# Reordering the mixer of a two-layer decoder step: conv half of the out product first, the S5 half last

## The chip, the cores and the metric

The kernel runs on one core of a Trainium2 chip. The metric is the device time of one execution in microseconds (us), the median of several runs. TensorE (PE in the profile) does the matrix products, VectorE (DVE) and ScalarE (ACT) the elementwise work, GpSimd (POOL) some copies and tables; SyncE (SP) and POOL issue the transfers.

## The reference, cut to what matters

Two layers over 288 token columns (a prompt of 256 and 8 samples of 4 tokens), model width 2048. The part of a layer that the change touches is the mixer:

```python
z = x @ w_in
u = z[..., :S5_WIDTH]
cv = z[..., S5_WIDTH:S5_WIDTH + CONV_WIDTH]
cg = z[..., S5_WIDTH + CONV_WIDTH:]
y5, h_re, h_im = _s5(u, h0_re, h0_im, ...)
g5 = jax.nn.gelu(y5.astype(x.dtype))
s5_out = g5 * jax.nn.sigmoid(g5 @ s5_w_glu)
c = cv * jax.nn.sigmoid(cg)
c, new_conv = _causal_dwconv(c, conv_buf, conv_w, conv_b)
c = jax.nn.silu(_ln(c, conv_ln_g, conv_ln_b))
mix = jnp.concatenate([s5_out, c], axis=-1) @ w_out
x = _ln(ALPHA * x + mix, ln1_g, ln1_b)
```

`_s5` is a scan over a diagonal complex state (64 groups); the convolution is 31 taps deep, its LayerNorm runs over all 1024 conv channels. A ConvFFN and an embedding stage follow, which the change leaves alone. All data are float32.

## The kernel before, in words

Tokens lie along the free dimension, features along the 128 partitions: `x32`, `xh` and `xl` are 16 tiles of 128 x 288 each. Every product is made of **blocks**: one 128 x 128 piece of a weight matrix times one such tile. Weights stream from memory in units of eight blocks (`wraw`, 512 KB); ACT and DVE split each unit into a high and a low part (`whi`, `wlo`), the activations are split the same way (`xh`, `xl`), and a block is three matmuls: whi·xh, whi·xl, wlo·xh (L369, L374, L375). A layer has 3104 blocks in the order of the table that `layer_phases` writes; the host packs the weights in that order, so PE, the splits and the weight transfers all follow it.

In the mixer the table runs: `u0` (64 blocks, the first four of eight chunks of `u`), then for each conv chunk j the pair `p{j}` (32 blocks: values and gates), with `v{j}` (16 blocks, one more chunk of `u`) behind p1 to p4, then `g` (64 blocks, the GLU product) and `o` (256 blocks, the whole out product, 16 columns over all 16 input tiles). I number the blocks of a layer from its start: u0 0 to 64, p0 64 to 96, p1 96 to 128, and so on.

Around them `mixer` writes out by hand:

* **The convolution of chunk j.** When p{j} is done, DVE makes the gated rows in `cbuf`; POOL writes them to memory (`cb_d`), loads the taps (`cw`) and reads the rows back in 32-row windows (`stack`, four transfers), writes them to the output (`out_dram<-cbuf`), and loads the next chunk's `cbuf`. There is one `cbuf`, one `cw` and one `stack`, so each waits for the last reader of the one before; the last chunk's `stack` is read by SP instead. `conv(j)` (64 small matmuls, L1105 and L1108) runs one chunk later, after p{j+1}; conv(7) after the first 32 blocks of `g`.
* **The S5 scan**, a background generator in steps: per chunk an injection (`bu`), a kernel product (`kps`), the scan on DVE, a projection (`y`), then GELU, a round through memory (`y_d`, back to `u32`) and a split. Its transfers (`ust`, `sqb`, `tm`, `k_d`, `y_d`) are issued by SP and POOL in program order between weight loads. Where its steps stand is decided while the program is written, by a clock `pe_t` that counts an assumed time for each block and each step of a convolution; `wait` and `at` put a step some thousand of these nanoseconds later.
* **The LayerNorm over the conv chunks** (`ln_finish`, then a pipeline of `ln_sub`, `c_norm`, `c_silu` and split per chunk): before, its small DVE chain has 24 blocks of `g` beside it, and the eight chunks' work the last of `g` and the first 40 blocks of `o`, which read the GLU's outputs.

`G_CUT = (32, 40, 64, 64)` says how `g` is cut around conv(7) and the LayerNorm. The GELU'd chunks lie in `xh[8..15]` before, the GLU's outputs in `xh[0..7]`; the conv half takes `xh[8..15]` after `g` has read them.

Of the kernel before, what the change touches and what calls it, by code (L numbers as in the profile page):

```python
# [7 lines left out]
F32 = mybir.dt.float32  # L8
F32R = mybir.dt.float32r
I32 = mybir.dt.int32  # L10
AF = mybir.ActivationFunctionType
OP = mybir.AluOpType

P = 128
DM = 2048
KD = DM // P
# [3 lines left out]
TOK = SEQ + NB * NT  # L20
# [6 lines left out]
CVC = 8  # L27
# [5 lines left out]
ALPHA = (2.0 * DEPTH) ** 0.25  # L33
# [8 lines left out]
STEP = 4  # L42
# [23 lines left out]
LOOK = 1  # L66
EV_GAP = 10
NATIVE = 10
G_CUT = (32, 40, 64, 64)
U_AT = {1: [4], 2: [5], 3: [6], 4: [7]}  # L70

PRM = {}
_o = 0
# [12 lines left out]
def _order(mat, ms, ks, g):  # L86
    ms, ks = list(ms), list(ks)
    out = [(mat, k, m) for k in ks for m in ms[:g]]
    for m in ms[g:]:
        out += [(mat, k, m) for k in ks]  # L90
    return out


def layer_phases():
    ph = [("u0", _order("w_in", range(4), range(KD), 4))]
    for j in range(CVC):
        ph.append((f"p{j}", _order("w_in", [8 + j, 16 + j], range(KD), 0)))
        if j in U_AT:
            ph.append((f"v{j}", _order("w_in", U_AT[j], range(KD), 0)))
    ph.append(("g", _order("s5_w_glu", range(8), range(8), 4)))  # L100
    ph.append(("o", _order("w_out", range(KD), range(KD), 5)))
    for z, ms in enumerate(EPARTS[:3]):
        ph.append((f"e{z}", _order("pe_w", ms, range(PEK), 0)))
    j0 = 0
    for h, n in enumerate(FH):
        ms = [m for j in range(j0, j0 + n) for m in (j, FF + j)]
        ph.append((f"up{h}", _order("ffn_w_up", ms, range(KD), 5 if h == 0 else 0)))
        ks = list(range(j0, j0 + n))
        dn = [("ffn_w_down", k, m) for m in (0, 1) for k in ks[:-2]]
        dn += [("ffn_w_down", k, m) for m in (0, 1) for k in ks[-2:]]  # L110
        dn += _order("ffn_w_down", range(2, KD), ks, 0)
        ph.append((f"dn{h}", dn))
        j0 += n
    for z, ms in enumerate(EPARTS[3:]):
        ph.append((f"e{3 + z}", _order("pe_w", ms, range(PEK), 0)))
    ph.append(("pg", _order("pe_w_gate", range(KD), range(KD), 5)))
    return ph
# [36 lines left out]
class Core:  # L154
# [188 lines left out]
    def run(self, blocks, xs, evac, sums=None, wide=False):  # L343

        nc = self.nc
        tot, seen, accs = sums or self.sums(blocks)
        k0, pend = blocks[0][1], []
        for _, k, m in blocks:
            if pend and k != k0:
                for out, w, xl in pend:  # L350
                    nc.tensor.matmul(out, w, xl, start=False, stop=False)  # L351
                pend = []
            w = self.next_block()
            if m not in accs:
                if wide and len(accs) == 4:
                    accs[m] = (1 << 30, self.ps.tile([P, 512], F32, tag="one", name="acc5", bufs=1))
                else:
                    t = self.acc_tile()
                    accs[m] = (self.acc_n, t)
            out = accs[m][1][:, :TOK]  # L360
            n = seen[m]
            first, last = n == 0, n == tot[m] - 1
            if len(w) == 1:
                self.pe_t += 485.0
                nc.tensor.matmul(out, w[0], self.x32[k], start=first, stop=last)
            else:
                xh, xl = xs(k)
                self.pe_t += 369.0
                nc.tensor.matmul(out, w[0], xh, start=first, stop=False)  # L369
                if k == k0 and not last and (pend or not seen[m]):  # L370
                    nc.tensor.matmul(out, w[1], xh, start=False, stop=False)  # L371
                    pend.append((out, w[0], xl))
                else:
                    nc.tensor.matmul(out, w[0], xl, start=False, stop=False)  # L374
                    nc.tensor.matmul(out, w[1], xh, start=False, stop=last)  # L375
            seen[m] += 1
            if last:
                a, t = accs.pop(m)
                self.evq.append((a, lambda m=m, t=t: evac(m, t[:, :TOK])))
            if self.evq and self.pos - self.ev_pos >= EV_GAP:  # L380
                self.evict()
        while self.evq:
            self.evict()
# [157 lines left out]
    def xs(self, k):  # L541
        self.need(k)
        return self.xh[k], self.xl[k]
# [507 lines left out]
    def mixer(self, l, ph):  # L1051
        nc, a = self.nc, self.a
        V = self.V
        with self.tc.tile_pool(name="mx", bufs=1) as mp:
# [3 lines left out]
            scan = self.scan = self.start(self.s5(l, mp), 0.0)  # L1058
# [8 lines left out]
            cst = self.ln_begin(CVC * P)  # L1067
# [19 lines left out]
            gsplit = set()  # L1087

            def split_g(force=False, n=S5C):
                while n and self.gdone and (force or self.gdone[0][1] <= self.pe_t):  # L1090
                    c = self.gdone.pop(0)[0]
                    self.split_x(8 + c, self.u32[c])
                    gsplit.add(c)
                    n -= 1

            def conv(j):
                st, cw = stacks.pop(j)
                o = self.acc_tile()
                for k in range(8):
                    self.tick()  # L1100
                    self.pe_t += 640.0
                    if j == CVC - 2 and k >= 4:
                        split_g(n=1)
                    for b in range(4):
                        nc.tensor.matmul(o[32 * b:32 * b + 32, :SEQ], cw[:, b, k], st[:, b, 4 * k:4 * k + SEQ],  # L1105
                                         start=(k == 0), stop=False, tile_position=(0, 32 * b))
                    for b in range(4):
                        nc.tensor.matmul(o[32 * b:32 * b + 32, SEQ:TOK], cw[:, b, k], window(st, b, CW + 4 * k),  # L1108
                                         start=False, stop=(k == 7), tile_position=(0, 32 * b))
                nc.scalar.activation(cvo[j], o[:, :TOK], AF.Identity, bias=self.prm("conv_b", j))  # L1110
                self.ln_acc(cst, cvo[j], j == CVC - 1)

            for j in range(CVC):
# [26 lines left out]
                if j:  # L1140
                    conv(j - 1)
                while "done" not in part:
                    self.late.pop(0)[1]()
                stack(j)
                if j in U_AT:
                    self.run(ph[f"v{j}"], self.xs, ev_u)

            def xs_g(k):
                split_g()
                while k not in gsplit:  # L1150
                    self.step(scan)
                    self.run_timed(True)
                    split_g(True)
                return self.xh[8 + k], self.xl[8 + k]
            def ev_g(m, acc):
                t = mp.tile([P, TOK], F32, tag="cvt", name="gt", bufs=3)
                nc.scalar.activation(t, acc, AF.Tanh, scale=0.25)
                w = mp.tile([P, TOK], F32, tag="cvt", name="gt", bufs=3)
                V.scalar_tensor_tensor(w.rearrange("p (n s) -> p s n", s=STEP),
                                       t.rearrange("p (s n) -> p s n", s=STEP), 1.0,  # L1160
                                       self.u32[m].rearrange("p (s n) -> p s n", s=STEP), op0=OP.add, op1=OP.mult)
                self.split_x(m, w, 0.25)
            sums = self.sums(ph["g"])
            self.run(ph["g"][:G_CUT[0]], xs_g, ev_g, sums)
            self.finish(scan)
            conv(CVC - 1)

            def fill(z):
                self.run(ph["g"][G_CUT[z]:G_CUT[z + 1]], xs_g, ev_g, sums)
            fill(0)  # L1170
            self.flush()
            self.ln_finish(cst, lambda z: z and fill(z), keep=True)
            th = {}

            def c_norm(j):
# [6 lines left out]
            def c_silu(j):  # L1182
# [2 lines left out]

            self.lazy(self.pipeline(CVC, ((0, lambda j: self.ln_sub(cst, cvo[j])), (1, c_norm), (2, c_silu),
                                          (3, lambda j: self.split_lo(8 + j, cvo[j], 0.5)))))
            if G_CUT[2] < G_CUT[3]:
                fill(2)
            self.load_p(l, mp)  # L1190
            st = self.ln_begin(DM)

            def xs_o(k):
                self.need(min(k - 3, 7) - LOOK)
                return self.xh[k], self.xl[k]

            def ev_o(m, acc):
                V.scalar_tensor_tensor(self.x32[m], self.x32[m], 1.0 if m == KD - 1 else ALPHA, acc,
                                       op0=OP.mult, op1=OP.add)
                self.ln_acc(st, self.x32[m], m == KD - 1)  # L1200
                if m == 6:
                    self.ln_pre(st, self.x32[KD - 1], ALPHA)
            self.run(ph["o"], xs_o, ev_o, wide=True)
        return st

    def load_p(self, l, mp):
# [307 lines left out]
```

## Time and profile before

| | |
|---|---|
| median of 3 runs | 2792.56 us (2791.43 to 2795.7) |
| the profiled execution's own time | 2793.7 us |
| its span, first to last instruction | 2791.9 us |
| PE busy in the span | 2684.0 us (96%) |
| DVE, ACT, POOL busy | 65%, 48%, 11% |
| mean granted TensorE clock | 0.984 of full speed |
| memory traffic | 463.27 MB read, 20.68 MB written |

A row of the "windows" view gives for a stretch of time how long each engine was busy in it and with how many instructions, the granted clock (1.00 is 2.4 GHz, 0.50 is 1.2 GHz), the busy share of the sixteen DMA engines and GB/s. In a row of the timeline the square bracket is the idle time of the engine just before, and what ended it. Layer one of the profile runs from 0 to about 1388 us, layer two from there; the first mixer ends near 415, the second near 1806.

### The profile page before, as it was taken

What the parts mean: (1) busy time and instruction counts of PE and PEld (TensorE: products, weight loads), DVE (VectorE), ACT (ScalarE), POOL (GpSimd) and SP (SyncE); (2) the same over time, 40 slices, a digit from 0 to 9 for tenths busy, and PEclk for the clock granted to TensorE, in tenths of its full rate; (3) what the DMA queues carried; (4) which work ended last, traced back from release to release, by engine and by line L of the source; (5) the groups of instructions that cost most, each with busy time, mean ns of one, the idle gap of its engine ahead of it and who ended that gap; (6) DMA issues with size and microseconds to landing.
All of it is one profiled execution on the core that took longest, in us unless ns stands there. A gap on an engine that the chain in (4) does not pass through costs nothing. (4 is left out here: it accounts for less than half of the span.)

```text
span 2791.9 us, 57891 instructions
## 1 busy us (share of the span) xinstructions
PE 2684.0 (96%) x23696; PEld 2623.0 (94%) x23696; DVE 1815.6 (65%) x3017; ACT 1353.2 (48%) x2224; POOL 304.3 (11%) x923
## 2 busy tenths in 40 slices
PE   8889999999999999999889879999999999999997
PEld 7778999999999999999888769999999999999997
DVE  6875768664566456667778747676645664566686
ACT  3444547553455345536454435475534553455363
POOL 3442001000000000000115410010000000000000
PEclk9999999999999999999999999999999999999998
DMA  7887544554455544544468874445555455455543
GB/s 238 240 237 224 171 152 164 162 181 163 158 168 164 180 159 157 181 162 151 145 197 242 225 206 156 150 161 165 180 166 162 159 179 171 150 173 171 166 152 102
DMA packets 175609, 487.72 MB, mean 175 GB/s; under 512 B 37616, under 2 KB 61696, under 8 KB 175344
## 3 DMA queue, kind: packets, MB, share of 16 engines
q1 hardware_dynamic: 160832, 434.56, 48.6%
q0 software_dynamic: 14512, 49.47, 6.4%
q8 instruction: 186, 3.05, 0.4%
q14 instruction: 79, 0.65, 0.1%
HBM read 463.27 MB, written 20.68 MB: 173 GB/s over the span
## 5 line engine op out<-in xcount | busy, mean ns | idle before, releaser
L369 PE MATMUL acc<-xh,whi 128*128 128x288 f32 x4656 | 1389.3, 299 | 13.0 <-ACT xh L528 5.1
L374 PE MATMUL acc<-xl,whi 128*128 128x288 f32 x4357 | 1289.7, 296 | 0.6 <-DVE xl L140 0.2
L375 PE MATMUL acc<-xh,wlo 128*128 128x288 f32 x4357 | 1284.3, 295 | 0.5 <-issue 0.5
L195 ACT ACTIVATE whi<-wraw 128x1024 fp32r<-128x1024 f32 x766 | 791.4, 1050 | 350.5 <-PE acc L374 220.4
L140 DVE TENSOR_TENSOR wlo<-wraw,whi 128x1024 fp32r<-128x1024 f32 x766 | 918.6, 1223 | 28.6 <-issue 12.5
L369 PEld LDWEIGHTS acc<-xh,whi 128*128 128x128 f32 x4656 | 876.5, 188 | 20.5 <-ACT xh L528 5.4
L374 PEld LDWEIGHTS acc<-xl,whi 128*128 128x128 f32 x4357 | 821.4, 189 | 3.7 <-DVE xl L140 2.1
L375 PEld LDWEIGHTS acc<-xh,wlo 128*128 128x128 f32 x4357 | 823.8, 189 | 0.7 <-issue 0.7
L140 DVE SCALAR_TENSOR_TENSOR fo<-fe,parf,fo 128x304 f32<-128x304 f32 x352 | 188.2, 535 | 354.2 <-ACT fo L1250 347.9
L369 PE MATMUL acc<-hh,whi 128*128 128x288 f32 x1408 | 416.4, 296 | 0.0
L374 PE MATMUL acc<-hl,whi 128*128 128x288 f32 x1312 | 387.7, 296 | 0.0
L375 PE MATMUL acc<-hh,wlo 128*128 128x288 f32 x1312 | 387.4, 295 | 0.0
L369 PEld LDWEIGHTS acc<-hh,whi 128*128 128x128 f32 x1408 | 264.9, 188 | 0.1
L375 PEld LDWEIGHTS acc<-hh,wlo 128*128 128x128 f32 x1312 | 247.2, 188 | 0.0
L374 PEld LDWEIGHTS acc<-hl,whi 128*128 128x128 f32 x1312 | 247.0, 188 | 0.0
L1246 ACT ACTIVATE fe<-acc 128x256 f32<-128x256 f32 x176 | 67.6, 384 | 301.1 <-PE acc L375 301.1
L1256 POOL COPY fstage<-fe 128x9 f32<-128x9 f32 x176 | 42.2, 240 | 1035.3 <-ACT fe L1247 1024.5
L428 ACT ACTIVATE ln_q<-x 128x288 f32<-128x288 f32 x90 | 40.2, 446 | 221.0 <-DVE x L140 221.0
L140 DVE TENSOR_TENSOR x<-x,acc 128x288 f32<-128x288 f32 x64 | 29.1, 454 | 144.7 <-PE acc L375 144.7
L1250 ACT ACTIVATE fo<-fe,parf 128x304 f32<-128x304 f32 x176 | 113.0, 642 | 16.5
L1270 ACT ACTIVATE hh<-fth 128x288 fp32r<-128x288 f32 x88 | 39.2, 445 | 162.9 <-DVE fth L140 162.9
L140 DVE SCALAR_TENSOR_TENSOR x<-x,acc 128x288 f32<-128x288 f32 x64 | 29.0, 453 | 132.9 <-PE acc L375 132.9
(237 smaller groups left out, 2366.9 us busy)
## 6 DMA issues: line engine op xcount, KB each, us to landing
wraw<-in_wts_dram SPq DMA_DIRECT2D x776, 512.0 KB
stack<-cb_d POOLq DMA_DIRECT2D x56, 282.0 KB, 8.8
cw<-in_convw_dram POOLq DMA_DIRECT2D x16, 512.0 KB, 5.7
cbuf<-in_convi_dram POOLq DMA_DIRECT2D x16, 283.5 KB, 4.5
cb_d<-cbuf POOLq DMA_DIRECT2D x16, 283.5 KB, 4.0
out_dram<-cbuf POOLq DMA_DIRECT2D x16, 283.5 KB, 10.4
tm<-k_d SPq DMA_DIRECT2D x64, 64.0 KB
sbt<-in_s5b_dram SPq DMA_DIRECT2D x14, 256.0 KB
```

The source lines that it names most:

```text
L140: return f(out, *args, **kw)
L195: self.nc.scalar.activation(hi, self.raw[s], AF.Copy)
L369: nc.tensor.matmul(out, w[0], xh, start=first, stop=False)
L374: nc.tensor.matmul(out, w[0], xl, start=False, stop=False)
L375: nc.tensor.matmul(out, w[1], xh, start=False, stop=last)
L428: nc.scalar.activation(st["q"], v, AF.Square)
L1246: nc.scalar.activation(e[:, 2:2 + SEQ], acc[:, :SEQ], AF.Copy)
L1250: nc.scalar.activation(o[:, :w], e[:, 2:EW], AF.Identity, bias=self.prm("ffn_conv_b", m), scale=self.prm("ffn_conv_w2", m))
L1256: nc.gpsimd.tensor_copy(stage[:, z, :, 0], e[:, SEQ:EW:6])
L1270: nc.scalar.activation(hh[i], h, AF.Copy, scale=0.5)
```

## The change

* `u` chunks 4, 5 and 6 follow p1, p2 and p5; chunk 7 (`vz`, 16 blocks) follows p7 and conv(6). conv(7) stands inside `vz`, after its sixth block, the LayerNorm's sums after its ninth.
* The out product is in two: `oc` (128 blocks, input tiles 8 to 15, the conv half) right after `vz`, then `g`, then `os` (128 blocks, the S5 half). `oc` adds into `alpha * x` (`ev_c`), `os` adds its result (`ev_s`): 16 more 128 x 288 additions per layer.
* The S5 chunk that takes its input from `vz` runs beside `oc`. The GELU'd chunks go to `xh[0..7]` and all eight are split where `g` begins, the GLU's outputs to `xh[8..15]`.
* `pe_t` counts 400 for a block (was 369) and 500 for a step of a convolution (was 640).

```diff
-G_CUT = (32, 40, 64, 64)
-U_AT = {1: [4], 2: [5], 3: [6], 4: [7]}
+U_AT = {1: [4], 2: [5], 5: [6]}
+U_END = 7
+V_CUT = (6, 9)
...
+    ph.append(("vz", _order("w_in", [U_END], range(KD), 0)))
+    ph.append(("oc", _order("w_out", range(KD), range(8, KD), 5)))
     ph.append(("g", _order("s5_w_glu", range(8), range(8), 4)))
-    ph.append(("o", _order("w_out", range(KD), range(KD), 5)))
+    ph.append(("os", _order("w_out", range(KD), range(8), 5)))
...
-                self.pe_t += 369.0
+                self.pe_t += 400.0
...
-                    self.split_x(8 + c, self.u32[c])
+                    self.split_x(c, self.u32[c])
...
-                    self.pe_t += 640.0
-                    if j == CVC - 2 and k >= 4:
-                        split_g(n=1)
+                    self.pe_t += 500.0
...
+            vz = ph["vz"]
+            vsum = self.sums(vz)
+            self.run(vz[:V_CUT[0]], self.xs, ev_u, vsum)
+            conv(CVC - 1)
+            self.run(vz[V_CUT[0]:V_CUT[1]], self.xs, ev_u, vsum)
+            self.flush()
+            self.ln_finish(cst, lambda z: z and self.run(vz[V_CUT[1]:], self.xs, ev_u, vsum), keep=True)
...
+            def ev_c(m, acc):
+                V.scalar_tensor_tensor(self.x32[m], self.x32[m], ALPHA, acc, op0=OP.mult, op1=OP.add)
+            self.run(ph["oc"], xs_c, ev_c, wide=True)
...
-                self.split_x(m, w, 0.25)
-            sums = self.sums(ph["g"])
-            self.run(ph["g"][:G_CUT[0]], xs_g, ev_g, sums)
+                self.split_x(8 + m, w, 0.25)
+            self.run(ph["g"], xs_g, ev_g)
             self.finish(scan)
-            conv(CVC - 1)
-
-            def fill(z):
-                self.run(ph["g"][G_CUT[z]:G_CUT[z + 1]], xs_g, ev_g, sums)
-            fill(0)
-            self.flush()
-            self.ln_finish(cst, lambda z: z and fill(z), keep=True)
...
-            def ev_o(m, acc):
-                V.scalar_tensor_tensor(self.x32[m], self.x32[m], 1.0 if m == KD - 1 else ALPHA, acc,
-                                       op0=OP.mult, op1=OP.add)
+            def ev_s(m, acc):
+                V.tensor_tensor(self.x32[m], self.x32[m], acc, OP.add)
                 self.ln_acc(st, self.x32[m], m == KD - 1)
...
-            self.run(ph["o"], xs_o, ev_o, wide=True)
+            self.run(ph["os"], lambda k: (self.xh[8 + k], self.xl[8 + k]), ev_s, wide=True)
```

What the table does to the engines' order is seen at three places of the second layer. The first is PE where the LayerNorm's last product (L510, L513 after the change) stands; `xh_102` is input tile 15, `xh_87` tile 0, `xh_95` tile 8. Before:

```order
L369 MATMUL acc<-xh_102,whi 128x288
L374 MATMUL acc<-xl_118,whi 128x288
L375 MATMUL acc<-xh_102,wlo 128x288
L510 MATMUL acc<-ln_dg,ones_120 128x288
L369 MATMUL acc<-xh_87,whi 128x288
L371 MATMUL acc<-xh_87,wlo 128x288
```

After:

```order
L378 MATMUL acc<-xh_101,wlo 128x288
L372 MATMUL acc<-xh_102,whi 128x288
L377 MATMUL acc<-xl_118,whi 128x288
L378 MATMUL acc<-xh_102,wlo 128x288
L513 MATMUL acc<-ln_dg,ones_120 128x288
L372 MATMUL acc<-xh_95,whi 128x288
L374 MATMUL acc<-xh_95,wlo 128x288
```

Before, the block behind that product reads a GLU output; now it reads conv chunk 0 after its normalisation.

The second is ACT around the LayerNorm's two copies (`ln_s<-acc`, L515 and L518); `gt` is the GLU's gate, `cvo` a conv chunk, `u_7` the last chunk of u. Before:

```order
L1157 ACTIVATE gt<-acc 128x288
L528 ACTIVATE xh_94<-gt 128x288
L515 ACTIVATE ln_s_20348<-acc 128x288
L515 ACTIVATE ln_s_20350<-acc 128x288
L1212 ACTIVATE phi<-p_20354 128x576
L195 ACTIVATE whi<-wraw 128x1024 x2
L1177 ACTIVATE cvo_16260<-ln_d,par 128x288
```

After:

```order
L1111 ACTIVATE cvo_16299<-acc,par 128x288
L431 ACTIVATE ln_q<-cvo_16299 128x288
L198 ACTIVATE whi<-wraw 128x1024
L1065 ACTIVATE u_7_16291<-acc 128x288
L518 ACTIVATE ln_s_19945<-acc 128x288
L518 ACTIVATE ln_s_19947<-acc 128x288
L198 ACTIVATE whi<-wraw 128x1024
L1160 ACTIVATE cvo_16292<-ln_d,par 128x288
L1162 ACTIVATE ln_d<-cvo_16292 128x288
L1160 ACTIVATE cvo_16293<-ln_d,par 128x288
L1162 ACTIVATE ln_d<-cvo_16293 128x288
L531 ACTIVATE xh_95<-cvo_16292 128x288
```

The copy of conv(7)'s result (`cvo_16299`), the LayerNorm and the first high part of the conv half (`xh_95`) now follow each other with two weight splits between them and no GLU work.

The third is POOL's queue behind conv(2), where `stack` of chunk 3 is read. Before:

```order
L1078 DMA stack<-cb_d 32x4x564 x4
L1080 DMA out_dram<-cbuf 128x567
L1064 DMA u_d_18349<-u_6_16258 128x288
L1115 DMA cbuf<-in_convi_dram 128x567
L864 DMA k_d<-kp 128x224
L926 COPY hin<-h_16275 128x4x8 x2
```

After:

```order
L1081 DMA stack<-cb_d 32x4x564 x4
L1083 DMA out_dram<-cbuf 128x567
L1116 DMA cbuf<-in_convi_dram 128x567
L867 DMA k_d<-kp 128x224
L929 COPY hin<-h_16307 128x4x8 x2
L889 TENSOR_TENSOR stb<-tix,fint 128x288
```

Chunk 6 of u has left this place with its 16 blocks; the load of the next `cbuf` now stands right behind the write that it has to wait for, and the S5 pieces behind it.

## Rows read from the trace of the kernel before

**Rows 1.** Windows: layer one from conv(0) to conv(7), and layer two's ConvFFN.

```profile
45.00:281.26 236.26, 208.50 (x3342) 188.61 (x3340) 167.57 (x291) 102.15 (x192) 98.12 (x172) 0.96 0.83 239
1810.00:2662.00 852.00, 852.00 (x6396) 851.51 (x6396) 514.47 (x766) 420.65 (x669) 48.38 (x267) 1.00 0.51 166
```

**Rows 2.** Windows, layer one: from conv(2) to conv(7), one row a chunk.

```profile
150.37:184.43 34.06, 30.66 (x562) 27.90 (x561) 26.46 (x45) 14.99 (x28) 12.59 (x25) 0.95 0.85 231
184.43:220.07 35.64, 29.64 (x449) 26.97 (x448) 28.00 (x49) 16.65 (x33) 19.60 (x30) 0.90 0.75 220
220.07:242.03 21.96, 20.63 (x402) 18.52 (x401) 13.72 (x26) 8.83 (x16) 6.16 (x15) 1.00 0.87 241
242.03:262.04 20.01, 18.95 (x321) 17.31 (x321) 7.37 (x11) 7.59 (x15) 4.26 (x9) 1.00 0.82 247
262.04:281.26 19.22, 17.33 (x225) 15.48 (x225) 9.30 (x17) 6.21 (x12) 3.24 (x6) 1.00 0.83 218
```

**Rows 3.** Windows, layer two: from conv(2) to conv(7), one row a chunk.

```profile
1525.47:1558.27 32.80, 30.03 (x514) 27.25 (x513) 26.91 (x51) 15.17 (x30) 15.89 (x28) 0.95 0.86 243
1558.27:1595.36 37.09, 31.92 (x561) 28.88 (x560) 28.18 (x47) 14.59 (x28) 12.42 (x25) 0.90 0.84 229
1595.36:1619.47 24.11, 21.00 (x401) 18.56 (x400) 19.17 (x35) 11.24 (x22) 10.81 (x20) 1.00 0.77 217
1619.47:1647.78 28.31, 20.69 (x322) 18.72 (x321) 7.55 (x11) 8.10 (x15) 5.84 (x13) 0.88 0.76 209
1647.78:1671.84 24.06, 18.93 (x225) 16.81 (x225) 11.33 (x22) 9.52 (x19) 2.70 (x5) 0.92 0.73 207
```

**Rows 4.** Waits of PE, 1560 to 1700 us: total us, times, longest.

```profile
PE y L389 <- DMA wraw<-in_wts_dram: 7.6, 1, 7.6
...
PE acc L369 <- ACT xh L528: 5.1, 1, 5.1
...
PE acc L369 <- ACT ln_s L515: 0.8, 1, 0.8
```

**Rows 5.** Chain that ended last, around conv(7) of layer two: start, us, what.

```profile
1652.91 7.66 DMA stack<-cb_d
1660.59 7.21 DMA u<-y_d
```

**Rows 6.** Timeline of PE: the first matmuls of conv(7) in layer one.

```profile
281.26 0.64 PE L1105 MATMUL acc<-stack,cw 128*32 128x256 f32 x8 [1.29 <-DMA stack<-cb_d]
```

**Rows 7.** Windows with L1105's matmuls alone: conv(6) of layer one.

```profile
262.04:266.30 4.26, 4.10 (x64) 1.30 (x64) 1.00 0.59 185
```

**Rows 8.** Timeline of POOL: loads of cbuf behind a write of it.

```profile
240.24 0.56 POOL L1115 DMA_DIRECT2D cbuf<-in_convi_dram  x1 [10.06 <-DMA out_dram<-cbuf]
1640.20 0.56 POOL L1115 DMA_DIRECT2D cbuf<-in_convi_dram  x1 [12.34 <-DMA out_dram<-cbuf]
```

**Rows 9.** Windows: two stretches at the lower clock, each behind a long wait.

```profile
1637.20:1643.90 6.70, 3.65 (x98) 3.49 (x99) 0.00 (x0) 0.49 (x2) 0.56 (x1) 0.50 0.79 223
1667.90:1674.60 6.70, 6.19 (x52) 4.36 (x56) 3.30 (x7) 2.85 (x8) 0.00 (x0) 0.50 0.10 42
```

**Rows 10.** Timeline of DVE and ACT: the conv LayerNorm of layer two.

```profile
1683.77 0.16 DVE L140 TENSOR_SCALAR ln_ne<-acc 96x6 f32<-96x6 f32 x1 [0.83 <-PE acc L459]
...
1686.30 0.45 DVE L140 SCALAR_TENSOR_TENSOR ln_dg<-ident,ln_n 96x288 f32<-96x288 f32 x1
1686.67 1.22 DVE L140 TENSOR_TENSOR wlo<-wraw,whi 128x1024 fp32r<-128x1024 f32 x1
...
1701.89 0.45 DVE L140 TENSOR_TENSOR ln_d<-cvo,ln_s 128x288 f32<-128x288 f32 x1
...
1704.39 0.43 ACT L528 ACTIVATE xh<-cvo 128x288 fp32r<-128x288 f32 x1
```

**Rows 11.** Lines of PE, 1440 to 1806 us: injections and the projections' second half.

```profile
L389 PE MATMUL y<-hin,om 128*32 128x72 f32 x512 | 15.6, 256 | 0.0
...
L389 PE MATMUL bu<-ust,em 128*32 128x72 f32 x448 | 10.6, 242 | 8.2 <-DMA ust<-u_d 5.2 <-ACT em L815 3.0
```

More of the change, by code (lines that the diff above doesn't have):

```diff
@@ L1146, in mixer @@
                     self.run(ph[f"v{j}"], self.xs, ev_u)
[L1148 to L1161, printed above, removed]
-                self.split_x(m, w, 0.25)
-            sums = self.sums(ph["g"])
-            self.run(ph["g"][:G_CUT[0]], xs_g, ev_g, sums)
-            self.finish(scan)
+            vz = ph["vz"]
+            vsum = self.sums(vz)
+            self.run(vz[:V_CUT[0]], self.xs, ev_u, vsum)
             conv(CVC - 1)
-            def fill(z):
-                self.run(ph["g"][G_CUT[z]:G_CUT[z + 1]], xs_g, ev_g, sums)
-            fill(0)
+            self.run(vz[V_CUT[0]:V_CUT[1]], self.xs, ev_u, vsum)
             self.flush()
-            self.ln_finish(cst, lambda z: z and fill(z), keep=True)
+            self.ln_finish(cst, lambda z: z and self.run(vz[V_CUT[1]:], self.xs, ev_u, vsum), keep=True)
             th = {}
@@ L1187, in mixer, with xs_c, xs_g, ev_g @@
                                           (3, lambda j: self.split_lo(8 + j, cvo[j], 0.5)))))
-            if G_CUT[2] < G_CUT[3]:
-                fill(2)
+            def xs_c(k):
+                self.need(k - 8)
+                return self.xh[k], self.xl[k]
+            def ev_c(m, acc):
+                V.scalar_tensor_tensor(self.x32[m], self.x32[m], ALPHA, acc, op0=OP.mult, op1=OP.add)
+            self.run(ph["oc"], xs_c, ev_c, wide=True)
+            def xs_g(k):
+                split_g()
+                while k not in gsplit:
+                    self.step(scan)
+                    self.run_timed(True)
+                    split_g(True)
+                return self.xh[k], self.xl[k]
+            def ev_g(m, acc):
+                t = mp.tile([P, TOK], F32, tag="cvt", name="gt", bufs=3)
+                nc.scalar.activation(t, acc, AF.Tanh, scale=0.25)
+                w = mp.tile([P, TOK], F32, tag="cvt", name="gt", bufs=3)
+                V.scalar_tensor_tensor(w.rearrange("p (n s) -> p s n", s=STEP),
+                                       t.rearrange("p (s n) -> p s n", s=STEP), 1.0,
+                                       self.u32[m].rearrange("p (s n) -> p s n", s=STEP), op0=OP.add, op1=OP.mult)
+                self.split_x(8 + m, w, 0.25)
+            self.run(ph["g"], xs_g, ev_g)
+            self.finish(scan)
             self.load_p(l, mp)
             st = self.ln_begin(DM)
-            def xs_o(k):
-                self.need(min(k - 3, 7) - LOOK)
-                return self.xh[k], self.xl[k]
-            def ev_o(m, acc):
-                V.scalar_tensor_tensor(self.x32[m], self.x32[m], 1.0 if m == KD - 1 else ALPHA, acc,
-                                       op0=OP.mult, op1=OP.add)
+            def ev_s(m, acc):
+                V.tensor_tensor(self.x32[m], self.x32[m], acc, OP.add)
                 self.ln_acc(st, self.x32[m], m == KD - 1)
                 if m == 6:
-                    self.ln_pre(st, self.x32[KD - 1], ALPHA)
-            self.run(ph["o"], xs_o, ev_o, wide=True)
+                    self.ln_pre(st, self.x32[KD - 1])
+            self.run(ph["os"], lambda k: (self.xh[8 + k], self.xl[8 + k]), ev_s, wide=True)
         return st
```

## Prediction

> **What bounds the kernel now.** I read the page's slices first. From layer one's end of the mixer to the second mixer PE is always busy at full clock, and the windows view of layer two's ConvFFN shows 852 us of work in 852 us: 6396 matmuls, 0.133 us each, so a block of three costs 0.40 us, and the DMA engines are half idle there [rows 1]. All idle time and all lower clock lie in the two mixers. In layer one from conv(0) to conv(7) PE is busy for 208.5 of 236.3 us, the clock averages 0.96, and the DMA engines are busy 83% of the time at 239 GB/s [rows 1]. So that stretch is paced by transfers as much as by PE, and what an edit does to it is read chunk by chunk.
>
> The windows by chunk say what a chunk takes with and without 16 blocks of `u` in it. With them: 32.8 to 37.1 us. Without: 21.96 and 20.01 in layer one, 24.11 and 28.31 in layer two [rows 2, 3]. The last row of each group, conv(6) to conv(7), is 19.2 and 24.1 us, with 32 blocks of `g` in it. The longest of layer two's rows holds the longest wait of PE, 7.6 us before a projection [rows 3, 4]. The waits also show `g` standing 5.1 us for a GELU'd chunk, and the chain of waits says why: `u<-y_d` landed 7.2 us after the `stack` ahead of it [rows 4, 5]. The LayerNorm costs PE one wait of 0.8 us [rows 4].
>
> The next thing read is what conv(7) stands on. There is one `stack`, so its reload starts when conv(6) has ended. In layer two conv(6) began at 1647.78; the reload began at 1652.91 and landed at 1660.59, 12.8 us after conv(6)'s start [rows 3, 5]. In layer one conv(7) itself waited for it, 19.2 us after conv(6)'s start [rows 2, 6]. Before, 32 blocks of `g`, 12.8 us, and a projection covered that.
>
> Last, the price of a long wait beyond itself: behind two of them the granted clock is 0.50, the lower level (1.2 GHz); 3.65 us of PE's work in one such stretch and 6.19 in the other were done at half speed [rows 9]. Half of it was lost: 1.8 to 3.1 us, 2.5 as a mean.
>
> **The change part by part.** The total of blocks is the same. Work leaves the stretch before conv(7) and stands behind it.
>
> *Chunks conv(2) to conv(7).* Of their five rows two now lose 16 blocks of `u` (behind conv(2) and conv(3)), and one gains 16 (behind conv(4)). For a row without them the trace has 22 to 28.3 us. Layer one I take at 24, near its own 22. For layer two I take 28, its upper end, since POOL's queue there holds what the scan needs: the load of `cbuf` waits 10.06 and 12.34 us behind the write of it [rows 8], POOL works in order, and in the order after the change the kernel spectrum's store (`k_d`), the copies of the state and the tables stand behind that load. The chunk with `v5` is 21.96 + 16 x 0.40 = 28.4. The next, with its S5 work thinned, is layer one's 20.0. From conv(6) to conv(7) PE has only conv(6), 4.1 us [rows 7], a projection, 15.6/8 = 1.95 [rows 11], and six blocks, 2.4: 8.5 us in all, against 12.8 and 19.2 for `stack`. I take the transfers to last as long as now: 16 us, the mean, a new wait of 7.5 us (4.3 to 10.7).
> Layer one: 24 + 24 + 28.4 + 20 + 16 = 112.4, now 34.06 + 35.64 + 21.96 + 20.01 + 19.22 = 130.9: -18.5.
> Layer two: 28 + 28 + 28.4 + 20 + 16 = 120.4, now 32.80 + 37.09 + 24.11 + 28.31 + 24.06 = 146.4: -26.0. The waits of 7.6 and 5.1 us [rows 4] go with it.
>
> *Behind conv(7).* Now 32 blocks of `g` and 256 of `o` follow it; afterwards 10 of `vz`, 128, 64 and 128, that is 42 more: +16.8. Chunk 7's injection (10.6/7 = 1.5) and projection (1.95) come along: +3.5 [rows 11]. The wait for conv(7) brings a stretch at the lower clock: +2.5 [rows 9].
>
> *The LayerNorm.* Its small chain on DVE runs from 1683.77 to the end of `ln_dg`, 3.0 us [rows 10]; the seven blocks of `vz` left beside it are 2.8, so nothing to speak of. But `oc` begins with conv chunk 0 normalised, where now eight inputs from the GLU stand ahead. From DVE's subtraction (1701.89) to the end of the high part (1704.39 + 0.43) it is 2.9 us in the trace; ACT's copy of the product stands ahead of that, an operation of the size of the high part's 0.43. So 3.3 us at least. The order puts weight splits between, 1.22 us on DVE each [rows 10]; with two of them and a second copy it is some 6.2. I take 4.5, in place of 0.8: +3.7. Part of a lower-clock stretch follows, under the 2.5 above since the wait is shorter: +1.7. The other seven chunks follow at DVE's and ACT's pace while `oc` runs at 0.40 us a block; they were as fast before, beside blocks that did not wait for them, and each new input serves several columns of `oc` at once (`wide`), so I charge no more.
>
> *From `oc` to `g` to `os`.* The first GELU'd chunks need chunk 7's projection, which stands some 70 blocks into `oc`, 28 us ahead of `g`: hidden; if the clock of the steps put it at the end of `oc`, the 7.2 us of `u<-y_d` [rows 5] would show. `g` to `os` has the split of the last GLU output to wait for: 1.2 us (one split of weights ahead of it on DVE). The sixteen additions of 0.45 us, 7.2 a layer, lie on DVE under `oc`'s 51 us of PE, half of which DVE has free: nothing. If DVE were full there, they would cost up to 7.2.
>
> Behind conv(7), layer one: 16.8 + 3.5 + 2.5 + 3.7 + 1.7 + 1.2 = +29.4. Layer two has now a lower-clock stretch there of its own, whose part behind conv(7)'s start goes: +28.0.
>
> *Sum.* (-18.5 + 29.4) + (-26.0 + 28.0) = 10.9 + 2.0 = +12.9. On the profiled execution's own 2793.7 us that is 2806.6, and as that execution lies 1.1 us above the median, **2805 us** for the median.
>
> The DMA side gives the same direction. The two layers move about 20 us of PE work each to where PE is the bound and take a like share of transfers out of the stretch where transfers are; the two cancel, and what is left over are the new waits.
>
> **A rule against this sum.** The new wait of 7.5 us rests on 7.66 us for the reload of `stack` [rows 5], under an 83% busy memory system. The Trainium skill, "DMA: Bandwidth & Descriptors", section "Anatomy of one DMA — SWDGE (gpsimd) path", gives a transfer 2.0 us fixed plus its bytes at 436 GB/s. For the four pieces of `stack` (32 x 4 x 564 floats each, 1.15 MB together) an estimate by that page is 4.6 us, which 1.95 + 2.4 of PE's work would all but cover. The trace disagrees by three microseconds, and by far more in layer one; by the page the sum would lose the 7.5 and the 2.5 behind it in each layer.
>
> **Rivals.**
> *A, no wait at conv(7) (faster).* The stack's reload lands within 8.5 us of conv(6)'s start in both layers. For it: less is under way there, since the 32 blocks of weights behind conv(6) are now 6 and the S5 chunk is away. Against: the layers show 12.8 and 19.2. The page weighed above would have it so. It takes 2 x (7.5 + 2.5) = 20 off: 2785. It decides once the reload lands under 10 us after conv(6)'s start in both layers.
> *B, short chunks.* Rows without `u` cost 22 in both layers, as layer one's third row does: -4 and -12 in the sum, 2789. For it: nothing but blocks and a conv needs to be there. Against: layer two's 24.1 and 28.3.
> *C, the S5 half is what paces.* The same scan steps are now squeezed into fewer blocks, so the chunks without `u` don't shrink but wait for the state, `k_d` or tables behind POOL's 10 to 12 us [rows 8]: 32 us in place of 24 in layer one and 28 in layer two, two chunks each: +16 + 8, and the shorter waits of layer two return only in part: 2820 to 2829.
>
> **How the numbers follow.** Forecast 0.45, A 0.17, B 0.2, C 0.18. What a measurement can tell from no change is 0.2%, 5.6 us: faster is under 2787, slower above 2798. A and the lower part of B are faster (0.17 + 0.08), the rest of B is the same with a tenth of the forecast's lower end, and C and most of the forecast are slower: 0.25, 0.2, 0.55. The forecast's own bounds: 4.3 to 10.7 for the wait at conv(7), 22 to 28.3 for a chunk, 3.3 to 6.2 for `oc`'s start. Those are -6.4, -4 - 12 and -2.4 on the lower side, +6.4, +9 and +3.4 on the upper; not all at one end at once, as a root of squares they give -15 and +12: 2790 to 2817. The range reaches to A below and to C's beginning above: 2785 to 2821.
>
> **What would show it.** In the profile after: a wait of conv(7)'s first matmul for `stack<-cb_d` of 4 to 11 us in both layers and a clock of 0.50 behind it; conv(2) to conv(3) and conv(3) to conv(4) of 22 to 28 us, with PE's waits for `wraw` or the S5 pieces; one wait of `oc`'s first matmul for `xh`, 3.3 to 6.2 us; `oc`, `g` and `os` without idle time else. A stretch from conv(7) to the end of the mixer of some 163 us in place of 134 would confirm the second half of the sum. The prediction is wrong if PE finds `stack` there (A), if the v-less chunks stand at 30 and more with waits for `tm`, `hin` or `ust` (C), or if `g` waits for the last chunk of the scan, which the sum calls hidden.

## The result, and the profile after

The changed kernel takes 2874.41 us (median; 2871.33 to 2876.37), the kernel before 2792.35 beside it: a ratio of 1.0291, 95% interval 1.0273 to 1.0308. The forecast was 2805, at most 2821. The direction was right, but of the 82 us of loss 69 were not in the sum.

The profiled execution took 2871.33 us, its span is 2869.2, so 77.3 us more than the span before. Both views of the two mixers are cut at the starts of the convolutions, as [rows 2, 3] are. PE, PEld (the loads of its weights), DVE, ACT and POOL follow each other in a row. First the windows of layer one, from conv(2) to conv(7), the last row from conv(7) to the end of the mixer (the LayerNorm's last product):

```profile
151.28:172.94 21.66, 21.24 (x417) 19.36 (x416) 20.53 (x38) 11.33 (x23) 8.82 (x14) 1.00 0.81 230
172.94:206.59 33.65, 22.48 (x434) 20.85 (x436) 17.85 (x33) 11.55 (x22) 14.46 (x27) 0.94 0.87 229
206.59:231.37 24.78, 24.78 (x283) 22.64 (x273) 9.82 (x13) 9.54 (x16) 5.46 (x10) 0.95 0.89 236
231.37:253.76 22.39, 18.84 (x305) 16.98 (x304) 14.28 (x28) 8.37 (x15) 5.82 (x10) 1.00 0.81 235
253.76:272.56 18.80, 8.77 (x243) 7.52 (x243) 8.78 (x14) 5.51 (x11) 7.53 (x13) 0.86 0.76 212
272.56:463.17 190.61, 166.68 (x1374) 160.20 (x1374) 116.91 (x218) 76.87 (x124) 5.02 (x12) 0.92 0.38 127
```

The same of layer two:

```profile
1573.79:1597.73 23.94, 22.22 (x401) 20.01 (x400) 17.78 (x32) 8.73 (x19) 8.05 (x15) 0.93 0.85 237
1597.73:1622.47 24.74, 22.63 (x402) 21.09 (x401) 20.43 (x38) 10.46 (x21) 9.59 (x18) 0.93 0.84 240
1622.47:1649.07 26.60, 26.14 (x386) 23.87 (x385) 12.65 (x25) 13.55 (x25) 10.66 (x22) 1.00 0.90 245
1649.07:1675.46 26.39, 21.37 (x305) 19.21 (x305) 16.18 (x31) 8.54 (x15) 6.47 (x11) 0.87 0.84 248
1675.46:1693.02 17.56, 8.50 (x243) 6.75 (x243) 7.71 (x12) 5.39 (x11) 7.53 (x13) 0.83 0.69 196
1693.02:1883.56 190.54, 167.39 (x1374) 161.09 (x1374) 116.89 (x218) 76.87 (x124) 5.00 (x12) 0.91 0.39 127
```

The last rows carry it. The stretch from conv(7) to the end of the mixer was, before, in layer one and in layer two:

```profile
281.26:415.33 134.07, 132.03 (x1089) 129.40 (x1089) 95.33 (x178) 67.34 (x107) 0.17 (x3) 1.00 0.49 161
1671.84:1805.81 133.97, 132.93 (x1089) 129.37 (x1089) 94.43 (x177) 65.35 (x103) 0.17 (x3) 0.99 0.44 150
```

It is 190.6 and 190.5 us now, 56.5 more in each. Up to conv(7) layer one gained 8.7 us (272.56 for 281.26); layer two, from the end of the first mixer to conv(7), 26.7. Together 56.5 - 8.7 + 56.6 - 26.7 = +77.7.

The waits of PE behind conv(7) in layer one, 272 to 464 us (total, times, longest), name what is in those 190 us:

```profile
PE acc L372 <- DVE x L143: 10.9, 6, 1.9
PE acc L1106 <- DMA stack<-cb_d: 8.8, 1, 8.8
PE lnp L462 <- DVE ln_s L143: 7.0, 1, 7.0
PE acc L372 <- ACT xh L531: 3.9, 1, 3.9
PE acc L354 <- DVE xl L143: 1.0, 1, 1.0
```

The second and fourth are the two waits that the prediction speaks of, near their sizes (7.5 and 4.5 there). The first and third it does not have. `DVE x` is the addition of a finished column into `x32`, the operation that the prediction hid under PE's work: six times PE stood for one, three times in `oc`, three times in `os`. And before the LayerNorm's first product PE stood 7.0 us for its sums. Layer two has the same rows, 10.8 and 7.0. The timeline of DVE inside `oc` shows that DVE was not busy when PE waited for it:

```profile
340.53 1.23 DVE L143 TENSOR_TENSOR wlo<-wraw,whi 128x1024 fp32r<-128x1024 f32 x1 [3.66 <-issue]
341.68 0.44 DVE L143 SCALAR_TENSOR_TENSOR x<-x,acc 128x288 f32<-128x288 f32 x1
347.31 1.23 DVE L143 TENSOR_TENSOR wlo<-wraw,whi 128x1024 fp32r<-128x1024 f32 x1 [5.19 <-issue]
348.45 1.18 DVE L143 SCALAR_TENSOR_TENSOR x<-x,acc 128x288 f32<-128x288 f32 x3
```

DVE stood idle for 3.7 and 5.2 us, made a weight split, and only then the addition: the addition stood late in its program. DVE could not make it in its idle time, since the split ahead of it had to wait for PE. ACT's half of the first of these two splits shows it; it could begin when PE's last matmul before the wait was under way (that one started at 340.15):

```profile
340.35 1.06 ACT L198 ACTIVATE whi<-wraw 128x1024 fp32r<-128x1024 f32 x1 [4.20 <-PE acc L377]
```

So PE, the split and the addition stood in a row, and PE waited for both. The clock went with it; of the windows of three stretches behind conv(7), the two that hold those waits are at 0.87 and 0.78, the one between them is full:

```profile
336.00:362.00 26.00, 20.34 (x125) 19.73 (x126) 10.73 (x22) 7.42 (x14) 0.00 (x0) 0.87 0.27 88
424.00:463.20 39.20, 27.74 (x161) 26.48 (x161) 20.89 (x54) 10.31 (x19) 0.00 (x0) 0.78 0.18 59
362.00:424.00 62.00, 60.77 (x456) 60.42 (x454) 44.25 (x65) 29.67 (x45) 0.17 (x3) 1.00 0.52 175
```

**The theory** is in `run`, in lines that the diff leaves alone. A finished column is added once ten blocks have gone since the last addition (`EV_GAP = 10`), or when its accumulator is asked for again. In `o` a column is 16 blocks long. In `oc` and `os` it is 8. So columns finish faster than they are added, and the backlog (the finished columns that are not added yet) grows until a new column asks for a buffer whose addition has only just been put into DVE's program, behind a weight split: 1.23 + 0.44 us and the way there, 1.83. What is left over at the end of `os` is drained in one go, with the LayerNorm's three operations for each column behind it, and PE has nothing to do meanwhile. One rival takes the rows at their word: DVE has too much to do with sixteen more additions a layer. A second rival is the new step times, a third that the new wait at conv(7) with all that follows is larger than the windows tell.

### The profile page after: what moved, and what is told of

It reads as the page before. It is cut to its first block, busy times and chain, and to the rows that moved or that the text cites. A ratio compares the mean times of both kernels' runs of the same rounds, so it can differ in the third digit from the quotient of the medians.

```text
span 2869.2 us, 57990 instructions
## 1 busy us (share of the span) xinstructions
PE 2711.2 (94%) x23696; PEld 2650.6 (92%) x23696; DVE 1827.7 (64%) x3049; ACT 1356.2 (47%) x2224; POOL 307.2 (11%) x923
## 5 line engine op out<-in xcount | busy, mean ns | idle before, releaser
L143 DVE TENSOR_TENSOR x<-x,acc 128x288 f32<-128x288 f32 x96 | 42.9, 452 | 160.7 <-PE acc L378 160.7
L1106 PE MATMUL acc<-stack,cw 128*32 128x256 f32 x1024 | 76.0, 415 | 25.7 <-DMA stack<-cb_d 24.4
## 6 DMA issues: line engine op xcount, KB each, us to landing
out_dram<-cbuf POOLq DMA_DIRECT2D x16, 283.5 KB, 10.3
```

The source lines that it names most:

```text
L143: return f(out, *args, **kw)
```

## The experiments

**1. The pace of the additions.** Six blocks between two additions in `oc` and `os`, in place of ten.

```diff
-    def run(self, blocks, xs, evac, sums=None, wide=False):
+    def run(self, blocks, xs, evac, sums=None, wide=False, gap=EV_GAP):
...
-            if self.evq and self.pos - self.ev_pos >= EV_GAP:
+            if self.evq and self.pos - self.ev_pos >= gap:
...
-            self.run(ph["oc"], xs_c, ev_c, wide=True)
+            self.run(ph["oc"], xs_c, ev_c, wide=True, gap=6)
...
-            self.run(ph["os"], lambda k: (self.xh[8 + k], self.xl[8 + k]), ev_s, wide=True)
+            self.run(ph["os"], lambda k: (self.xh[8 + k], self.xl[8 + k]), ev_s, wide=True, gap=6)
```

> The changed kernel, with one number: in oc and os a finished column may be added after 6 blocks since the last addition (10 in the changed kernel, and 10 stays elsewhere). Theory 1 (a column of oc and os is 8 blocks long and an addition comes at most every 10 blocks, so additions fall behind until a buffer has to be waited for, three waits of 1.8 us in each of oc and os, and four columns are left for the end of os, 7.0 us before the LayerNorm's product): those waits go, and with them most of the lower clock behind them; 18 us of waiting in each layer and 6 to 10 of half clock, so 2874 falls by 45 to 56, to 2818 to 2830. Theory 2 (the sixteen more additions a layer and the shorter columns load DVE itself, and the waits only show it): the waits move to other columns, 2864 to 2878.

Measured: 2827.25 us, ratio to before 1.012 (1.0099 to 1.014), so 47 us less than the changed kernel. Its waits of PE from 269 to 441 us:

```profile
PE acc L1106 <- DMA stack<-cb_d: 9.7, 1, 9.7
PE acc L372 <- ACT xh L531: 4.0, 1, 4.0
PE lnp L462 <- DVE ln_s L143: 2.3, 1, 2.3
PE acc L354 <- DVE xl L143: 1.0, 1, 1.0
```

The six waits for an addition are gone, in both layers, and the one before the LayerNorm fell from 7.0 to 2.3. From conv(7) to the end of the mixer, layer one and layer two:

```profile
269.66:440.40 170.74, 163.38 (x1375) 158.73 (x1376) 117.71 (x218) 75.89 (x123) 3.77 (x12) 0.92 0.42 140
1670.98:1837.81 166.83, 159.12 (x1374) 153.87 (x1374) 116.58 (x218) 76.15 (x124) 5.01 (x12) 0.95 0.43 144
```

That is 19.9 and 23.7 us less than in the changed kernel, nearly all of the gain. As many additions are made on DVE as before the edit. Theory 1 holds; DVE's load does not explain it.

**2. Eight blocks**, the same edit with 8.

> The same with 8 blocks. Theory 1: the five first columns end together and from there one column ends for each addition, so the backlog neither grows nor shrinks: first waits for a buffer stay or come once a phase, and about as many columns are left for the end of os; 2835 to 2865, between 6 and 10. Theory 2: as with 10, 2864 to 2878.

Measured: 2827.38 us in one run. The expectation of a middle value missed. No wait for an addition is left in either layer; before the LayerNorm 4.2 us are. One addition for each column is enough for the buffers, and the five columns that end together at the start cost no wait.

**3 and 4. The step times alone**, each way.

```diff
-                self.pe_t += 369.0
+                self.pe_t += 400.0
...
-                    self.pe_t += 640.0
+                    self.pe_t += 500.0
```

> The kernel before with the step times of the change alone (400 for a block, 500 for a convolution's step). Theory 1 leaves nothing to the step times: 2780 to 2800. A rival, that the new step times put the S5 half's steps and transfers wrongly and cost the tens of microseconds: above 2820.

> The changed kernel with the step times of before (369 and 640). Theory 1: the waits in oc, os and before the LayerNorm don't hang on them, 2860 to 2885. The rival of the step times: below 2845.

Measured: the order of before with the new step times 2786.9 us, ratio 0.9978 (0.9966 to 0.999); the new order with the old ones 2880.94, ratio 1.031 (1.029 to 1.0329). In the old order the step times are a small gain, some 6 us; in the new order the difference is of the same size and way, but the interval of 1.031 overlaps that of the changed kernel (1.0273 to 1.0308). The rival falls: the new step times do not make the loss.

**5. The other way round: the old order made to fall behind.** In the kernel before, `o` (16 blocks a column) gets one number, `gap=18`. The same edit with 20, the ratio of 8 to 10, has no time: that program deadlocks, its engines waiting for each other.

> The kernel before with one number: in o a finished column may be added only 18 blocks after the last addition. Its columns are 16 blocks long, so the additions fall behind as in the changed kernel (8 blocks a column, 10 between additions), by two blocks a column. If that makes the loss, and not the order, the sixteen more additions or the step times, the old order gets the same picture in each layer: about three waits of 1.8 us for a buffer inside o, some 7 us before the LayerNorm's product, and lower clock behind them, 11 to 17 us a layer, 2814 to 2827. If falling behind is not the cause: 2790 to 2800.

Measured: 2835.6 us, ratio 1.016 (1.0132 to 1.0187), 44 us more and so above the bounds of either expectation. Its waits of PE from conv(7) of layer one on:

```profile
PE acc L369 <- DVE x L140: 7.3, 4, 1.8
PE lnp L459 <- DVE ln_s L140: 7.0, 1, 7.0
PE acc L369 <- issue: 0.9, 1, 0.9
PE acc L369 <- ACT ln_s L515: 0.8, 1, 0.8
```

The same two rows, with four waits of 1.8 us in `o` where `oc` and `os` have three each, and 7.0 us again. The old order, the old number of additions and the old step times show the picture once additions fall behind. By the median the price is 22 us a layer, more than the 11 to 17 expected. From conv(7) to the end of the mixer the trace has, in layer one and in layer two:

```profile
281.74:436.69 154.95, 138.68 (x1089) 134.49 (x1088) 96.15 (x178) 68.53 (x107) 0.17 (x3) 0.94 0.40 139
1685.11:1839.73 154.62, 139.28 (x1089) 134.65 (x1088) 95.24 (x177) 66.55 (x103) 0.17 (x3) 0.94 0.39 130
```

That is 20.9 and 20.7 us more than before, at a clock of 0.94 in place of 1.00 and 0.99. 14.3 of them are the two rows of waits, in either layer; PE is busy some 6.5 us longer with the same number of matmuls, which is the lower clock. The runs of this version lie far apart (2827.61 to 2840.4), and the profiled one is the fastest: its span is only 34 us longer than before's, since the stretch ahead of conv(7) of layer two was 8 us shorter in it.

**6 and 7. The wait at conv(7).** From here to experiment 11 every version has the pace of 6. A version with the pace of 6 and four columns together at the start of `oc` in place of five is the control for the move:

> Control for the next two: additions after 6 blocks as in the run before, and oc begins with four columns at once in place of five. Nothing else changes: 2822 to 2834.

Measured: 2827.07 us in one run, as expected. Then chunk 6 of `u` behind conv(6) too, so that 22 blocks stand before conv(7):

```diff
-U_AT = {1: [4], 2: [5], 5: [6]}
-U_END = 7
-V_CUT = (6, 9)
+U_AT = {1: [4], 2: [5]}
+U_END = [6, 7]
+V_CUT = (22, 25)
...
```

> The control, and chunk 6 of u moved from behind p5 into vz, so that 22 blocks stand between conv(6) and conv(7) where 6 did. If the wait for the stack's reload at conv(7) (9.7 and 10.3 us) and the lower clock behind it are costs of the position, they go, and the chunk behind conv(4) gives its 16 blocks back: 10 to 12 us in each layer, 2803 to 2810. If the reload is late because of the transfers around it and comes later still, the wait stays: 2822 to 2834.

Measured: 2830.66 us, ratio 1.0137 (1.012 to 1.0153): nothing gained. The windows of layer one from conv(5) to conv(6) and from there to conv(7), and then the waits from 225 to 445 us, show why:

```profile
225.54:249.75 24.21, 17.15 (x225) 15.55 (x225) 6.45 (x9) 6.08 (x9) 4.92 (x9) 0.95 0.86 237
249.75:269.59 19.84, 15.27 (x194) 12.71 (x195) 5.40 (x8) 4.09 (x6) 2.70 (x5) 0.84 0.70 195
```

```profile
PE acc L1106 <- DMA stack<-cb_d: 11.6, 2, 7.1
PE acc L372 <- ACT xh L531: 3.9, 1, 3.9
PE acc L377 <- DVE xl L143: 3.8, 2, 2.9
```

conv(7) still came 19.8 us after conv(6), with 22 blocks between them as with 6 (19.5 us in experiment 1). Its wait fell to 4.6 us, but conv(6) now waited 7.1 for its own `stack`. In layer two conv(7) came 17.5 us after conv(6), in experiment 1 18.8. So this chunk lasted as long as its rows took to go out and come back, with 22 blocks of work for PE as with 6; blocks moved into one chunk are missing in another. The part behind conv(7) grew by 7.3 us in layer one (163.85 for 156.52 from conv(7) to the LayerNorm's first product). 3.8 us of that are the third row, waits for low parts of the conv half that experiment 1 does not have; chunk 6's S5 work came along too, and its share was not measured apart.

**8. conv(7) seven blocks earlier, and seven blocks of `vz` behind the LayerNorm's product** (`V_CUT = (15, 18, 25)`, the rest run ahead of `oc`). In this version the last blocks of `vz` read input tiles that the first normalised conv chunks have already overwritten, so a part of chunk 7 is computed from other numbers.

> As the run before, but conv(7) after 15 of the 32 blocks, the LayerNorm's sums after 18, its last product after 25, and the last seven blocks stand between that product and oc. If oc's first wait (4.0 us in each layer, for the first normalised chunk) is the bare chain behind the product, it goes: 3 to 5 us a layer less than the run before if the wait at conv(7) stays away, 2796 to 2804; with conv(7) seven blocks earlier up to 3 us of its wait in a layer may come back. If DVE or ACT is what is full there, the wait only moves: as the run before.

Measured: 2847.25 us, ratio 1.0192 (1.0177 to 1.0207). `oc`'s first wait did not go, it grew to 5.3 us, and conv(7) waited 6.8 in layer one. It came 18.4 us after conv(6) in both layers, with 15 blocks between them, much the same length a third time. The version also shows a bound on this order: the conv half shares its tiles with the layer's input, so `oc` can't be prepared while `vz` reads them. Its price is not told apart here from that of the other moves, so the version settles nothing on the bare chain.

**9. Two buffers for `cbuf`.**

```diff
-                cb = mp.tile([P, CBW], F32, tag="cbuf", name="cbuf", bufs=1)
+                cb = mp.tile([P, CBW], F32, tag="cbuf", name="cbuf", bufs=2)
```

> The changed kernel with additions after 6 blocks and two buffers for cbuf, so that POOL's load of the next one no longer waits 10 to 12 us behind the write of the one before, with k_d, the state's copies and the tables queued behind it. If that queue sets the chunks without u (waits of 5.9 us for tm<-k_d, 6.7 for ust<-u_d), 6 to 15 us less over both layers: 2812 to 2821. If the transfers' rate sets them, the waits move elsewhere: 2822 to 2832.

Measured: 2821.53 us (2811.97 to 2827.92), ratio 1.01 (1.0072 to 1.0127): the interval overlaps that of experiment 1. In the traces conv(2) to conv(7) took 117.2 and 116.9 us, in experiment 1 119.3 and 119.4. In these two executions POOL's queue is worth some 2 us a layer; by the medians it is 6 us in all, which the scatter of this version's runs does not tell from nothing. The prediction's rival C gave it 8 us a chunk in layer one and 4 in layer two, 24 in all; even the fastest run is only 15 us below experiment 1's median.

**10. conv(7) without a reload of `stack`**, with chunk 6's rows in place of chunk 7's:

```diff
-                out = self.stack_tile(mp)
+                out = self.stack_tile(mp) if j < CVC - 1 else self.kept
+                self.kept = out
...
-                back(nc.gpsimd if j < CVC - 1 else nc.sync)
+                if j < CVC - 1:
+                    back(nc.gpsimd)
```

conv(7) then computes from other numbers; the version is there for its time alone.

> The changed kernel with additions after 6 blocks, and the reload of stack for the last conv chunk left out: conv(7) reads chunk 6's rows again (with chunk 7's taps), so part of the conv half is computed from other rows. It prices the wait at conv(7). If the new wait of 9.7 and 10.3 us and the lower clock behind it are what this placement costs, 2827 falls by 20 to 30, to 2797 to 2807. If something else is due at the same place (DVE's backlog, the scan, the weights), it takes the wait's place: 2815 to 2830.

Measured: 2814.37 us, ratio 1.0072 (1.0052 to 1.0092), 13 us less than experiment 1, short of the 20 to 30. The waits of PE from 255 to 440 us:

```profile
PE acc L1108 <- DMA cw<-in_convw_dram: 4.2, 1, 4.2
PE acc L372 <- ACT xh L531: 3.9, 1, 3.9
PE lnp L462 <- DVE ln_s L143: 2.3, 1, 2.3
```

The wait for `stack` is gone, and one of 4.2 us for the taps has taken its place: `cw` has one buffer as well, and its load starts when conv(6) has ended. So the reload is worth 13 us with the taps as they are; what the wait for the taps costs beyond that was not tried. And even with the reload gone the new order stays 0.7% behind the old one.

**11. A shorter chain to `stack`**: the gated rows of chunk 7 are made at once, and their write to the output follows conv(7).

```diff
-                    self.defer(2, glu)
+                    if j == CVC - 1:
+                        glu()
+                    else:
+                        self.defer(2, glu)
...
```

> The changed kernel with additions after 6 blocks, and a shorter chain to stack(7): the gated rows of chunk 7 are made as soon as p7 is done and not two blocks later behind the scan's steps on DVE, and the write of chunk 7's rows to the output comes after conv(7), out of the way of the reload. In the trace the rows were made some 6 us after conv(6)'s start and the reload took 10 us. If that chain sets conv(7), its wait falls by 2 to 5 us in each layer: 2816 to 2824. If the reload is held by all that is under way (weights, tm, the taps), 2824 to 2831.

Measured: 2822.41 us, ratio 1.0102 (1.008 to 1.0123), not told apart from experiment 1. The wait at conv(7) was 8.8 and 8.5 us, for 9.7 and 10.3. The gated rows came 4.4 us after conv(6)'s start, as without the edit (252.2 after 247.77; in experiment 1 254.5 after 250.12): DVE was busy without a gap from 244.9 to 252.2 with the scan and the splits that stood ahead. What little there is may come from the write that was taken out of the way; no run shows that alone.

**12. The old order with the new step times and two buffers for `cbuf`.**

> The order of before with the new step times and two buffers for cbuf: the version that the runs so far point to as the best. The step times alone gave 2786.9. If POOL's queue behind the load of cbuf costs anything in this order, 2778 to 2785; if not, 2785 to 2790.

Measured: 2785.65 us (2780.18 to 2790.94), ratio 0.9969 (0.9957 to 0.998). It beats both kernels; against the step times alone (0.9978) nothing can be told.

## Why the prediction was wrong, point by point

* **The step that failed** is that of `oc` to `os`: "The sixteen additions of 0.45 us, 7.2 a layer, lie on DVE under `oc`'s 51 us of PE, half of which DVE has free: nothing." That DVE has free time there was right, if nearer 40% than half (it was busy 38.6 of `oc`'s 64.6 us); "nothing" did not follow. Time on DVE was free, but an addition runs where the program puts it, and the program puts one in ten blocks. What has to be costed is not only the operations that a change adds, but how often each finished column comes up beside the pace at which the program takes them away: 16 blocks a column against 10 before, 8 against 10 after. Experiments 1 and 5 show it from both sides. Its price is 47 us of the 69 that were missing: 18 us of waiting in each layer (10.9 and 7.0, of which 2.3 stayed in experiment 1) and the lower clock behind it.
* **"`oc`, `g` and `os` without idle time else"** fell with it, and so did the 163 us from conv(7) to the end of the mixer: 190.6. With the pace mended it is 170.7 and 166.8 us, of which 2.3 are the LayerNorm's wait that stayed, and about 6 and 3 the slower blocks behind that wait (426.18 to 440.40 and 1826.41 to 1837.81, where before 8.3 us did). That is 36.7 and 32.8 more than before, where the sum had +29.4 and +28.0; without the two things named, which the sum does not have, it would be right within 1 us.
* **The wait at conv(7)**: forecast 4.3 to 10.7, taken as 7.5; measured 8.8 and 8.9. Where it comes from was only half seen. The prediction has the reload start at conv(6)'s end; in the changed kernel the way is longer: `cb_d` is written late (POOL issues it at 259.75, and it lands 3.8 us after that), SP issues the reload at 263.70, ten microseconds after conv(6)'s start, and conv(7) starts 8.9 us later. The row of SP's queue:

```profile
263.70 1.80 SPq L1081 DMA_DIRECT2D stack<-cb_d  x4
```

  The estimate of 4.6 us for these four pieces by the Trainium skill ("DMA: Bandwidth & Descriptors", "Anatomy of one DMA — SWDGE (gpsimd) path", a fit for transfers that GpSimd issues, while SP issues these) is half of the 8.9 us behind that row and 60% of the 7.7 before; the measurement decides. Rival A is out for this chain, and experiment 10 says that it would have been worth 13 us with the taps as they are, where it was put at 20.
* **The chunks**, conv(2) to conv(7). Layer two: -26.0 forecast, -27.1 measured. That sum is luck in part: its two chunks without `u` took 23.9 and 24.7 us for the 28 that were taken, conv(5) to conv(6) took 26.4 for 20, and the errors cancel. Layer one: -18.5 forecast, -9.6 measured. Of its rows one is off by far: conv(3) to conv(4), 33.65 us where 24 stood, with a wait of 6.5 us for `tm<-k_d` and one of 3.3 for `sqb<-q_d` in it. That is the prediction's own sign for rival C, in one of the four chunks without `u`. In experiments 1 and 9 the same two stretches of layer one, conv(2) to conv(4), still add up to 55 us. What sets this chunk in layer one was not tried further: two buffers for `cbuf` did not move it.
* **`oc`'s first wait**: 4.5 taken, 3.95 measured in both layers.
* **What stays open.** After the pace is mended 34 us remain between the orders, 22 more than the sum has. By the profiled execution of experiment 1 they are mostly layer one's: from conv(2) to conv(7) layer one gained 11.6 us and layer two 27.0, against the 36.7 and 32.8 behind conv(7). So some 7 of the 22 are layer one's chunks (11.6 gained for 18.5 forecast), and 7 and 5 stand behind conv(7). Experiments 6 to 8 show the reason for one chunk, conv(6) to conv(7): it lasts as long as its rows are on the way. That each of the other chunks has such a floor was argued from that, not shown.

## What to carry to other kernels

Where a change cuts accumulation groups shorter, compare how many blocks a group lasts with how many go by between two evacuations, and look at how many are left when the phase ends: a free engine does not help if its program puts the work late. In the trace this reads as PE waiting for a short operation of an engine that sat idle just before it. And where a stretch is paced by a round through memory, as conv(6) to conv(7) was here, moving PE's work out of it makes the rest longer and the stretch itself hardly shorter.

## What the runs showed of the hardware that was not expected

Waits of 1.83 us were not counted as long enough to matter to the clock, yet the stretch with three of them was at 0.87 (1.2 GHz for a part of it), with no wait longer than 1.83 us inside. Behind the first of the three, at 337.01, the clock stayed at 1.00; behind the second and the third it fell to the lower level:

```profile
337.00:342.27 5.27, 3.43 (x25) 3.24 (x25) 1.59 (x2) 1.06 (x1) 0.00 (x0) 1.00 0.31 101
342.27:345.70 3.43, 3.43 (x15) 3.43 (x16) 0.00 (x0) 0.00 (x0) 0.00 (x0) 0.51 0.41 153
349.04:352.50 3.46, 3.46 (x15) 3.46 (x16) 1.31 (x4) 0.00 (x0) 0.00 (x0) 0.52 0.46 156
```

The stretch behind it, from 362 to 424 us without such waits, was at 1.00. So was experiment 1, whose waits for an addition are gone, from 309 us in `oc` to the LayerNorm's first product at 426.18.
